# Slots 34 to 243 ordered by a list scheduler, solved in place in a ring of seven tiles

## The chip, the cores and the metric

The kernel runs on one core of a Trainium2 chip. The metric is the device time of one execution in microseconds (us). TensorE is called PE below, VectorE DVE, ScalarE ACT, GpSimd POOL and SyncE SP, as in the profile.

## The reference

```python
B, S, D = 16, 2048, 1024
xw = x @ w                              # x: B x S x D, w: D x D, float32
out[:, 0, :] = xw[:, 0, :]
for t in range(1, S):
    out[:, t, :] = decay[None, :] * out[:, t - 1, :] + xw[:, t, :]
```

A matrix product, and then along the time axis a decayed running sum with one decay for each of the 1024 columns.

## The kernel before, in words

**Tiling.** Time is cut into 64 chunks of 512 steps. Two chunks of one batch entry make a group, and the 1024 output columns are 8 tiles of 128. A *slot* is one group and one column tile: slot s = 8 * group + n, its result 128 columns by 1024 steps. A slot takes 16 matmuls of 128x512 on PE (8 blocks of the inner dimension, two chunks) into one of three PSUM tiles `ps0` to `ps2` of two banks each. Slots 0 to 247 are such; the last two chunks make 16 slots of half the length, so there are 264.

**Input.** A chunk is loaded in four quarters (`load`, L101) by DMAs that POOL issues, cast to bf16 on the way, into one of three `xb` tiles. DVE transposes the chunk in 32x32 blocks (`turn`, L110), one instruction of 128x2048, into one of two `xw` tiles. ACT copies it apart in two halves (`part`, L119; "X" and "Y" in the agenda) into one of five `xt` tiles, which PE reads. The quarters of later chunks wait in a list `loads`, which `turn_and_load` (L408) lengthens by those of chunk c + 3 when chunk c is turned.

**Solving a slot.** A *paired* slot halves the length of the serial scan:

- `copy` (p, ACT L183): PSUM to a tile `xs`, one of three
- `odd` (g, ACT L169): decay times the even steps, PSUM to a tile `h`, one of four
- `zero` (z, POOL L190 or ACT L192): the carry into column 1 of `so`, one of four
- `join` (j, POOL L196): odd steps of `xs` plus `h`, in place
- `scan` (S, DVE L201): 512 steps with decay squared, from `xs` into `so`
- `even` (h, ACT L169) and `fill` (c, POOL L246): the even steps, from `so` and `xs` into `so`
- `save` (k, ACT L250): the last step, for the same columns of the next group
- `back` (B, DVE L258): 32x32 transposes of `so` into a tile `ot`, one of four

A slot that is not paired has one DVE scan over all 1024 steps straight from PSUM (L221; D here), then save and back. Every fourth slot is of this kind (L149), apart from `flips`. Four slots, a *lump*, fill one `ot` tile; after the lump's last back, SP issues four stores of 512 KB.

A PSUM tile is free again when copy and odd have read it, or the long scan. So slot s + 3 cannot begin on PE before slot s has been read out.

**The order.** Each engine executes its instructions in the order in which the kernel writes them (`pin`). For slots 0 to 33 and the last 20 the order is written out by hand, slot by slot, in `agenda` (L447 to L503). For the slots between, `usual` (L514) writes the same pattern for every slot: pair of s, scans, completion of s - 1, backs of s - 2, then the turns and parts that `later` (L505 to L512) has put there, then one load or, if more than four are waiting, two. Slot 244 begins with `rest` (L528), which finishes slots 242 and 243.

Of the kernel before, what the change touches and what calls it, by code (L numbers as in the profile page):

```python
# [2 lines left out]

# [6 lines left out]
FP32 = mybir.dt.float32  # L10
BF16 = mybir.dt.bfloat16
ALU = mybir.AluOpType
# [13 lines left out]
def kernel(  # L26
# [26 lines left out]
    nc = tc.nc  # L53
    pin = tc.keep_in_program_order
    B, S, D = x.shape
    assert w.shape == (D, D)

    NQ = 4
    P = 32
    CQ = D // NQ  # L60
    K = CQ // P
    M = K // 2
    TL = 512
    NJ = TL // P
    NC = S // TL
    R = K // 2
    CH = D // 2
    CR = CH // NQ

    const = ctx.enter_context(tc.tile_pool(name="const", bufs=1))  # L70
    sb = ctx.enter_context(tc.tile_pool(name="sb", bufs=1))
# [4 lines left out]
    def ring(pool, name, count, shape, dtype=FP32):  # L76
        i = turns[name] = turns.get(name, -1) + 1
        return pool.tile(shape, dtype, name=f"{name}{i % count}")
# [13 lines left out]
    wcols = wsb.rearrange("p k (h r) q i -> p k h q r i", h=2)  # L92

    def ot_tile(nj):
        return ring(sb, "ot", 4, [128, nj, CR])

    xb_of = {}
    xw_of = {}
# [19 lines left out]

    def part(c, copy, m0, m1, j0=0, j1=NJ):  # L119
        if c not in xt_of:  # L120
            xt_of[c] = ring(sb, "xt", 5, [128, M, 2, TL], BF16)
        src = xw_of[c][:, m0:m1, j0:j1].rearrange("p m j i e -> p m e (j i)")
        pin(copy(out=xt_of[c][:, m0:m1, :, j0 * P:j1 * P], in_=src))  # L123

# [16 lines left out]
    class Tile:  # L141
# [3 lines left out]
        def __init__(self, g, n, ps, outlets):  # L145
            self.b, self.t0 = chunks[g[0]]
            self.T = TL * len(g)
            self.n, self.ps, self.outlets = n, ps, outlets
            self.paired = n % R != R - 1  # L149
            if len(tiles) in flips or len(tiles) - len(slots) in flips:  # L150
                self.paired = not self.paired
            self.turn = len(tiles)
            self.lot = sum(t.paired for t in tiles)
            self.prev = None if self.t0 == 0 else last[n]
            if self.t0 + self.T < S:
                last[n] = const.tile([128, 1], FP32, name=f"keep{n}", bufs=2)
                self.keep = last[n]
            else:
                self.keep = None

        @property
        def so(self):
            if not hasattr(self, "held"):
                self.held = sb.tile([128, 2 * TL + 2], FP32, name=f"so{self.turn % 4}")
            return self.held

        def decayed(self, src):
            h = ring(sb, "h", 4, [128, TL])[:, 0:self.T // 2]
            pin(nc.scalar.activation(  # L169
                out=h, in_=src, func=mybir.ActivationFunctionType.Copy,  # L170
                scale=dec[:, self.n:self.n + 1]))
            return h
# [6 lines left out]
                self.join()  # L179

        def copy(self):
            self.xs = sb.tile([128, 2 * TL], FP32, name=f"xs{self.lot % 3}")[:, 0:self.T]
            pin(nc.scalar.copy(out=self.xs, in_=self.ps))  # L183

        def odd(self):
            self.g = self.decayed(self.ps[:, 0:self.T:2])

        def zero(self):
            if self.prev is None:
                pin(nc.gpsimd.memset(self.so[:, 1:2], 0.0))  # L190
            else:
                pin(nc.scalar.copy(out=self.so[:, 1:2], in_=self.prev))  # L192

        def join(self):
            odds = self.xs[:, 1:self.T:2]
            pin(nc.gpsimd.tensor_tensor(out=odds, in0=self.g, in1=odds, op=ALU.add))  # L196

        def scan(self):
            T, n, so = self.T, self.n, self.so
            if self.paired:  # L200
                pin(nc.vector.tensor_tensor_scan(  # L201
                    out=so[:, 3:T + 2:2],
                    data0=squares[-1][:, n:n + 1].to_broadcast([128, T // 2]),
                    data1=self.xs[:, 1:T:2],
                    initial=0.0 if self.prev is None else self.prev,
                    op0=ALU.mult,
                    op1=ALU.add,
                ))
            else:
                parts = self.ps if isinstance(self.ps, tuple) else (self.ps,)  # L210
                size = T // len(parts)
                for i, ps in enumerate(parts):
                    self.run(ps, i * size, size)

        def run(self, ps, t, size):
            n, so = self.n, self.so
            if t:
                before = so[:, t + 1:t + 2]
            else:
                before = 0.0 if self.prev is None else self.prev  # L220
            pin(nc.vector.tensor_tensor_scan(  # L221
                out=so[:, t + 2:t + 2 + size],
                data0=dec[:, n:n + 1].to_broadcast([128, size]),
                data1=ps,
                initial=before,
                op0=ALU.mult,
                op1=ALU.add,
            ))
# [5 lines left out]
        def complete(self):  # L234
            if self.paired:
                self.even()
                self.fill()
            if self.keep is not None:
                self.save()

        def even(self):
            self.h = self.decayed(self.so[:, 1:self.T + 1:2])

        def fill(self):
            T = self.T
            pin(nc.gpsimd.tensor_tensor(  # L246
                out=self.so[:, 2:T + 2:2], in0=self.h, in1=self.xs[:, 0:T:2], op=ALU.add))

        def save(self):
            pin(nc.scalar.copy(out=self.keep, in_=self.so[:, self.T + 1:self.T + 2]))  # L250

        def back(self, half=None):
# [13 lines left out]
    class Outlet:  # L266


        def __init__(self, ns, nj, half=0, queues=(nc.sync,), pieces=1):
            self.pieces = pieces  # L270
            self.ns, self.missing, self.half = ns, set(ns), half
            self.nj, self.t0, self.queues = nj, half * nj * P, queues
            self.ot = ot_tile(nj)

        def store(self, b, t0):
            n0 = self.ns[0]
# [131 lines left out]
    def turn_and_load(c):  # L408
# [58 lines left out]
        18: "g16 T7 L h15 j16 p17 g17 B14 z17 c15 X7",  # L467
        19: "S16 j17 p18 B15 L g18 L S17 k16 h16 z18 j18",
        20: "Y7 S19 L c16 k17 h17 T8 k19 L c17",
        21: "p20 g20 L S18 X8 j20 B17 B19",  # L470
        22: "L h18 p21 c18 B16 k18 g21 B18 Y8 z20 L j21 S20",
        23: "p22 z21 z22 S21 L h20 g22 T9 c20 h21",
        24: "k21 k20 j22 S23 X9 L c21 Y9 B20 L",
        25: "B23 k23 p24 B21 g24 z24 j24 S22 z25",
        26: "p25 T10 k22 h22 g25 c22 S24 X10 j25",
        27: "B22 p26 S25 g26 z26 Y10 j26",
        28: "S27 h25 h24 c25 S26 c24",
        29: "B27 h26 c26 T11 p28 g28 j28 B24",
        30: "p29 B25 g29 z28 j29 S28 z29 S29",
# [22 lines left out]
        -1: "S-2 h-4 c-4 a-1 b-1 V",  # L502
    }  # L503
    flips = (1, 13, 15, -19, -18, -11, -8, -6, -3, -2)
    later = {}  # L505
    begun = {"T": 12, "X": 11, "Y": 11}
    for c in range(5, nch):
        first = c // 2 * K
        ahead = (7, 6, 4) if c % 2 else (11, 10, 8)
        for letter, a in zip("TXY", ahead):  # L510
            if c >= begun[letter]:
                later.setdefault(first - a, []).append(f"{letter}{c}")  # L512

    def usual(s):  # L514
        paired = [t.paired for t in tiles]
        do = [f"P{s}"] if paired[s] else []
        if paired[s - 1]:
            do.append(f"S{s - 1}")
        if not paired[s]:
            do.append(f"S{s}")  # L520
        do.append(f"C{s - 1}")
        if paired[s - 2]:
            do.append(f"B{s - 2}")
        if not paired[s - 1]:
            do.append(f"B{s - 1}")
        return do + later.get(s, []) + ["L"] * (2 if len(loads) > NQ else 1)

    def rest(s):  # L528
        do = [f"S{s - 1}"] if tiles[s - 1].paired else []
        do.append(f"C{s - 1}")  # L530
        if tiles[s - 2].paired:
            do.append(f"B{s - 2}")
        return do + [f"B{s - 1}"] + later.get(s, []) + ["L"] * len(loads)

    def perform(do):
        for deed in do:
            deeds[deed[0]](int(deed[1:] or 0))

    perform(agenda[-99].split())
    spares = [spare] + [ring(psp, "spare1", 1, [128, TL])]  # L540
    for step, (g, n) in enumerate(slots):
        T = TL * len(g)
        left = step - len(slots)
        if n % R == 0:
            ns, nj = range(n, n + R), T // P
            outlets = [Outlet(ns, nj)]
        if left == -R:
            outlets = []
        if step == 0:
# [48 lines left out]
            for k, l in todo:  # L598
                matmul(ps[:, l * TL:(l + 1) * TL], n, k, xt_of[g[l]])
        tiles.append(Tile(g, n, ps, outlets))  # L600
        do = agenda.get(step, agenda.get(left) if left >= -20 else None)
        if do is None:
            do = usual(step)
        else:
            do = do.split()
            if left == -20:
                do = rest(step) + do
        perform(do)
    assert not loads
# [1 line left out]
_INS = ['x', 'w', 'decay']  # L611
# [26 lines left out]
```

## Time and profile before

| | us |
|---|---|
| Median of 3 runs (lowest, highest) | 905.87 (905.47, 905.98) |
| The profiled execution's own time | 905.42 |
| Its span, first to last instruction | 903.5 |
| PE busy in the span | 892.3 |
| DVE, ACT, POOL busy | 825.5, 686.1, 657.2 |

In the profile, busy time is the time in which an engine executed at least one instruction. A group line names source line, engine, operation, what is written and read, the count, the busy time, the mean of one in ns, and the idle time ahead of it with what ended it. The timeline gives start, length and, in brackets, the idle time before an instruction and its releaser. The time from a DMA's issue to its landing is told by the views of one tile's instructions. An instruction often begins some 0.08 us before the recorded end of the one before it on the same engine.

### The profile page before, as it was taken

The numbers are of one execution on the slowest core, as the hardware profiler recorded it, in microseconds if no ns is written. First come the engines' busy times: TensorE is split into PE (matmuls) and PEld (weight loads), VectorE is DVE, ScalarE is ACT, GpSimd is POOL, SyncE is SP. The second block draws the span as 40 slices with busy tenths as digits, with TensorE's granted clock in tenths as the row PEclk, the third lists the DMA queues.
The fourth block names the chain that finished last, engine by engine and source line by source line (L and its number), as shares of the span: only waits on it lengthen the run. The fifth ranks groups of instructions, "written<-read, shape, count | busy, mean of one in ns | idle before, by whom it ended". The sixth has DMA issues, their size and how long they took to land.

```text
span 903.5 us, 11998 instructions
## 1 busy us (share of the span) xinstructions
PE 892.3 (99%) x4119; PEld 411.1 (45%) x4201; DVE 825.5 (91%) x628; ACT 686.1 (76%) x955; POOL 657.2 (73%) x755
## 2 busy tenths in 40 slices
PE   9999999999999999999999999999999999999997
PEld 5444444444444444444444444444444444444444
DVE  4999999999999999999998999999999999999997
ACT  4889867777877877877778778778777787787742
POOL 8888678777767768777677677787777776776632
PEclk9999999999999999999999999999999999999999
DMA  9999999999999999999999999999999999999868
GB/s 194 196 215 217 232 214 214 215 240 245 253 256 256 248 247 255 249 238 231 225 236 229 223 232 230 228 227 228 229 228 226 234 233 221 227 232 210 175 144 233
DMA packets 402542, 204.77 MB, mean 227 GB/s; under 512 B 8752, under 2 KB 401456, under 8 KB 402480
## 3 DMA queue, kind: packets, MB, share of 16 engines
q1 hardware_dynamic: 265168, 134.76, 61.1%
q0 software_dynamic: 137024, 68.70, 56.6%
q8 instruction: 33, 0.54, 0.2%
q10 hardware_dynamic: 288, 0.52, 0.2%
q14 instruction: 29, 0.24, 0.1%
HBM read 138.42 MB, written 134.22 MB: 302 GB/s over the span
## 4 chain that ended last, share of the span: by engine, by line
PE 94%; DMA 1%; DVE 1%; issue 1%; POOL 1%; ACT 0%; DVEq 0%; POOLq 0%
PE ps L131 94%; DMA ot<-in_w_dram 1%; DMA xb<-in_x_dram 1%; PE spare L131 1%; POOL xb L105 1%; DVE so L221 1%; POOL ot L299 0%; DVE xw L115 0%; ACT xt L123 0%; DVE ot L258 0%; PE spare L387 0%; DVE so L201 0%; DVE wsb L306 0%; ACT xs L183 0%; PE ps L387 0%
## 5 line engine op out<-in xcount | busy, mean ns | idle before, releaser
L131 PE MATMUL ps<-xt,wsb 128*128 128x512 bf16 x3942 | 863.5, 378 | 4.7 <-DVE wsb L306 0.3
L131 PEld LDWEIGHTS <-wsb 128*128 128x128 bf16 x4152 | 405.8, 98 | 480.0 <-ACT wsb L306 0.8
L196 POOL TENSOR_TENSOR xs<-h,xs 128x512 f32<-128x512 f32 (+1 forms) x190 | 242.9, 1278 | 189.5 <-ACT h L169 84.8
L183 ACT COPY xs<-ps 128x1024 f32<-128x1024 f32 (+1 forms) x190 | 189.4, 997 | 156.4 <-PE ps L131 146.2
L258 DVE STREAM_TRANSPOSE ot<-so 128x1024 f32<-128x1024 f32 (+1 forms) x260 | 300.1, 1192 | 3.1 <-POOL so L190 1.1
L246 POOL TENSOR_TENSOR so<-h,xs 128x512 f32<-128x512 f32 (+1 forms) x190 | 241.4, 1272 | 42.5 <-ACT h L169 27.9
L123 ACT COPY xt<-xw 128x2048 bf16<-128x2048 bf16 (+1 forms) x136 | 242.3, 1790 | 7.8 <-DVE xw L115 7.8
L105 POOL DMA_DIRECT2D xb<-in_x_dram x264 | 174.4, 662 | 3.2 <-DMA ot<-in_w_dram 1.0
L169 ACT ACTIVATE h<-so,dec 128x512 f32<-128x512 f32 (+1 forms) x190 | 145.4, 766 | 26.9 <-DVE so L201 23.7
L115 DVE STREAM_TRANSPOSE xw<-xb 128x2048 f32<-128x2048 f32 (+1 forms) x78 | 147.4, 1901 | 5.8 <-DMA xb<-in_x_dram 5.8
L201 DVE TENSOR_TENSOR_SCAN so<-spare,keep,xs 128x512 f32<-128x512 f32 (+1 forms) x97 | 120.0, 1240 | 27.5 <-POOL xs L196 27.2
L201 DVE TENSOR_TENSOR_SCAN so<-spare,xs 128x512 f32<-128x512 f32 x93 | 113.3, 1220 | 26.5 <-POOL xs L196 23.7
L169 ACT ACTIVATE h<-ps,dec 128x512 f32<-128x512 f32 (+1 forms) x190 | 130.2, 685 | 0.0
L221 DVE TENSOR_TENSOR_SCAN so<-dec,ps 128x1024 f32<-128x1024 f32 x34 | 76.8, 2261 | 1.0 <-ACT h L169 1.0
L221 DVE TENSOR_TENSOR_SCAN so<-dec,keep,ps 128x1024 f32<-128x1024 f32 (+1 forms) x35 | 76.0, 2171 | 0.2 <-issue 0.2
L250 ACT COPY keep<-so 128x1 f32<-128x1 f32 x136 | 25.4, 189 | 9.5 <-DVE so L221 9.0
L192 ACT COPY so<-keep 128x1 f32<-128x1 f32 x97 | 18.5, 191 | 2.5 <-DVE ot L258 2.3
L131 PE MATMUL ps<-xw,wsb 128*128 128x256 bf16 (+1 forms) x68 | 11.2, 301 | 0.0
L190 POOL MEMSET so<- 128x1 f32 x93 | 10.7, 116 | 0.6 <-DVE ot L258 0.6
L131 PE MATMUL spare<-xt,wsb 128*128 128x512 bf16 (+1 forms) x48 | 10.0, 335 | 0.0
L299 POOL DMA_DIRECT2D ot<-in_w_dram x12 | 6.6, 546 | 2.8 <-DMA xb<-in_x_dram 1.6
L324 PE MATMUL spare<-idle 128*128 128x512 bf16 x22 | 6.9, 488 | 1.2 <-DVE idle L314 1.2
(37 smaller groups left out, 36.5 us busy)
## 6 DMA issues: line engine op xcount, KB each, us to landing
out_dram<-ot SPq DMA_DIRECT2D x248, 512.0 KB, 10.9
xb<-in_x_dram POOLq DMA_DIRECT2D x248, 256.0 KB, 7.8
out_dram<-ot SPq DMA_DIRECT2D x12, 256.0 KB, 4.7
xb<-in_x_dram POOLq DMA_DIRECT2D x16, 128.0 KB, 5.6
ot<-in_w_dram POOLq DMA_DIRECT2D x12, 128.0 KB, 5.1
out_dram<-xb SPq DMA_DIRECT2D x3, 256.0 KB
ot<-in_w_dram ACTq DMA_DIRECT2D x2, 256.0 KB, 4.7
ot<-in_w_dram SPq DMA_DIRECT2D x2, 256.0 KB, 4.4
```

The source lines that it names most:

```text
L105: pin(nc.gpsimd.dma_start(out=xb_of[c][quad(q), j0:j1], in_=_ap(x, [[D, P], [P * D, j1 - j0], [1, CQ]], (b * S + t0 + j0 * P) * D + q * CQ)))
L115: pin(nc.vector.transpose(out=dst.rearrange("p (m j i) -> p j m i", m=M, i=P)[:, j0:j1, m0:m1], in_=src.rearrange("p (j m c) -> p j m c", ...
L123: pin(copy(out=xt_of[c][:, m0:m1, :, j0 * P:j1 * P], in_=src))
L131: pin(nc.tensor.matmul(out=ps[:, t0:t1] if ps.shape[1] >= t1 else ps, lhsT=lhs, rhs=rhs, start=(k == 0 and t0 == start), stop=(k == K - 1),))
L169: pin(nc.scalar.activation(out=h, in_=src, func=mybir.ActivationFunctionType.Copy, scale=dec[:, self.n:self.n + 1]))
L183: pin(nc.scalar.copy(out=self.xs, in_=self.ps))
L196: pin(nc.gpsimd.tensor_tensor(out=odds, in0=self.g, in1=odds, op=ALU.add))
L201: pin(nc.vector.tensor_tensor_scan(out=so[:, 3:T + 2:2], data0=squares[-1][:, n:n + 1].to_broadcast([128, T // 2]), data1=self.xs[:, 1:T:2 ...
L221: pin(nc.vector.tensor_tensor_scan(out=so[:, t + 2:t + 2 + size], data0=dec[:, n:n + 1].to_broadcast([128, size]), data1=ps, initial=befor ...
L246: pin(nc.gpsimd.tensor_tensor(out=self.so[:, 2:T + 2:2], in0=self.h, in1=self.xs[:, 0:T:2], op=ALU.add))
L250: pin(nc.scalar.copy(out=self.keep, in_=self.so[:, self.T + 1:self.T + 2]))
L258: pin(nc.vector.transpose(out=outlet.ot[:, :, c0:c0 + P], in_=self.so[:, 2 + t0:2 + t0 + nj * P].rearrange("p (i t) -> p i t", t=P)))
```

## The change

**Order.** Steps 34 to 243 are no longer written slot by slot. `steady` makes a `Job` for each piece of work: a quarter of a slot's matmuls, a copy, a scan, a load. A job has an engine, a cost, a key (when it is due, in us from the start of slot 34), and the jobs that it comes after. `in_order` then goes through time: whenever an engine has nothing to do, it gets the ready job with the lowest key. The jobs are emitted in order of these planned starts. The plan begins with all four engines idle at time 0. Its constants: 0.2158 us per matmul, 0.15 us from one engine to another, 19 us from a load's issue to its use, 13 us from a lump's last back to the free `ot` tile, and the costs in the dictionary below.

**Slots.** Every fifth slot (38, 43, ... 243) has the long scan; before it was every fourth (35, 39, ... 243). The code for `merged` groups has no effect: the tuple is empty, and every slot keeps its 16 matmuls.

**Turns and loads.** A chunk is turned in two DVE instructions of half the size (128 x 1024), each followed by its part on ACT. A load is planned no earlier than a slot after the one before it.

**Tiles.** `xs` is gone: copy, join, scan and fill work in `so`, which now has seven tiles. `xt` has four tiles in place of five, `ot` three in place of four, and these numbers hold for the whole kernel. An `ot` tile is taken at a lump's first back.

**Ahead of slot 34.** In the agenda, the parts of chunks 8 and 9 stand 1 to 3 steps later; those of chunk 10 have left step 26 and 27 for the scheduler. At slot 34 the scheduler also takes over scan, save, even, fill and back of slot 33 and the back of slot 32.

```diff
+    OTS, XTS, SOS, HS = 3, 4, 7, 4
+    FROM, TO = 34, 244
+    merged = ()
...
-        21: "p20 g20 L S18 X8 j20 B17 B19",
-        22: "L h18 p21 c18 B16 k18 g21 B18 Y8 z20 L j21 S20",
+        21: "p20 g20 L S18 j20 B17 B19",
+        22: "L h18 p21 c18 B16 k18 g21 B18 z20 L j21 S20",
         23: "p22 z21 z22 S21 L h20 g22 T9 c20 h21",
-        24: "k21 k20 j22 S23 X9 L c21 Y9 B20 L",
-        25: "B23 k23 p24 B21 g24 z24 j24 S22 z25",
-        26: "p25 T10 k22 h22 g25 c22 S24 X10 j25",
-        27: "B22 p26 S25 g26 z26 Y10 j26",
+        24: "X8 k21 k20 j22 S23 Y8 L c21 B20 L",
+        25: "B23 k23 p24 B21 g24 z24 j24 S22 X9 z25",
+        26: "p25 T10 k22 h22 g25 c22 Y9 S24 j25",
+        27: "B22 p26 S25 g26 z26 j26",
...
+    cost = {"p": 1.01, "g": .69, "z": .15, "j": 1.3, "S": 1.24, "D": 2.28, "h": .77, "c": 1.3,
+            "k": .19, "B": 1.21, "T": 1.19, "X": 1.9, "L": .66, "half": .585, "both": .68, "sum": 1.2, "wpool": 1.15, "wdve": .4, "slow": 4.2}
...
+        def chunk(c):
+            need = starts[c // 2] - 18 + (c % 2) * 12
+            if c > 11:
+                quads = [q for cc, q in loads if cc == c] if c <= 14 else range(NQ)
+                got = [Job("pool", cost["L"], need - 28 + 2.5 * q, lambda c=c, q=q: load(c, q),
+                           [turned.get(c - 3)]) for q in quads]
+                for q, a in zip(quads, got):
+                    a.early = max(0.0, need - 3 * 4 * each * R + 2 + q * each * R)
+                ends = [(a, LAND) for a in got]
+                for half in range(2):
+                    turned[c] = Job(
+                        "dve", cost["T"], need + 2 * half,
+                        lambda c=c, h=half: turn(c, 0, NJ, h * M // 2, (h + 1) * M // 2),
+                        ends + [turned.get(c - 1), part_of.get((c - 2, 1)), turned.get(c)])
+                    part_of[c, half] = Job(
+                        "act", cost["X"], need + 3 + 3 * half,
+                        lambda c=c, h=half: part(c, nc.scalar.copy, h * M // 2, (h + 1) * M // 2),
+                        [turned[c], part_of.get((c - 1, half))] + used.get(c - XTS, []))
...
+        def solve(tile, ready, key, banks):
...
+            gone = place.get((s - SOS, "B"))
...
+                end = pos("S", "dve", "D", 0, tile.scan, ready + [gone, prev])
...
+                    p = pos("p", "act", "p", 0, tile.copy, ready + [gone])
...
+                g = pos("g", "act", "g", .5, None, ready, True)
...
+                j = pos("j", "pool", "j", 1.2, tile.join, ready_xs + [g])
+                j.gives = (g,)
+                S = pos("S", "dve", "S", 1.5, tile.scan, [j, prev])
+                h = pos("h", "act", "h", 4.5, None, [S, z], True)
...
+                end = pos("c", "pool", "c", 4.4, tile.fill, [h])
...
+            if tile.kept:
+                pos("k", "act", "k", 3.7, tile.save, [place[s, "S"]])
+            back(tile, end, key)
...
+            b = Job("dve", cost["B"], key + 5, tile.back,
+                    [end, place.get((s, "k"))] + stored.get(lump - OTS, []) + ([first] if first else []))
...
+                last_one = Job("pe", each, t + q * each, do,
+                               [part_of.get((c, q // 2)) for c in g] + [last_one]
+                               + (after_ps[bank - 3] if bank >= 3 and q == 0 else []))
...
+        order = in_order()
+        for job in order:
+            job.do()
```

Of the built kernels, these stretches of each engine's order matter below (letters as above, numbers are slots; L, T and X with the chunk, its two parts a and b; L12 is issued in four quarters).

```
before, DVE   S33 B32 S34 D35 B33 B34 B35 S36 T12 S37 B36 S38 D39
after,  DVE   S33 B32 T12a B33 T12b S34 S35 B34 S36 B35 D38 S37 B36
before, ACT   p33 g33 h32 k32 p34 g34 h33 k33 X11a h34 k34 p36 g36 k35 X11b p37 g37
after,  ACT   p33 g33 h32 k32 X10a k33 h33 X10b p34 g34 X11a p35 g35 k34 h34 p36 g36 X11b k35 h35 p37 k36 g37
before, POOL  z32 j32 L12 L12 z33 j33 c32 L12 L12 z34 j34 c33 L13 L13 c34
after,  POOL  z32 j32 L12 L12 z33 j33 c32 L12 L12 L13 c33 z34 L13 j34 z35 L13 j35 c34 z36 j36 L13 c35
both,   DVE   D23 B20 B23 B21 S22 T10 S24 B22 S25 D27 S26 B27 T11 B24 B25 S28 S29 B26 B28 D31 S30 B29 B30 B31 S32 S33
```

## The prediction

> **What bounds the kernel now.** I read the page's busy line and the chain that ended last, then that chain in order of time.
>
> ```profile
> PE 892.3 (99%) x4119; PEld 411.1 (45%) x4201; DVE 825.5 (91%) x628; ACT 686.1 (76%) x955; POOL 657.2 (73%) x755
> ...
> PE 94%; DMA 1%; DVE 1%; issue 1%; POOL 1%; ACT 0%; DVEq 0%; POOLq 0%
> ```
>
> ```profile
> 47.87 10.74 PE ps L131 x49
> ...
> 69.67 10.74 PE ps L131 x49
> 80.46 10.74 PE ps L131 x49
> ...
> 857.67 10.74 PE ps L131 x49
> ```
>
> Piece by piece, from 41 to 868 us, the chain is PE alone: 50 matmuls (one record in 50 is missing) per 10.79 us, 0.2158 each, 3.453 a slot. PE never waits in slots 34 to 243, and the change leaves it every matmul. So there is **nothing to gain there**: the change is worth what it makes PE wait, and PE runs to the end, so every such microsecond is added. Slot 33 ends at 129.65 (its copy, waiting for PE, starts at 129.71); from there slot ends follow by 3.453.
>
> PE is covered by three PSUM tiles: slot s + 3 begins when copy and odd (or the long scan) of slot s are done. That is where I look for waits.
>
> **The steady part costs nothing, I estimate.** Pitches (start to start in the timelines): scan 1.14, long scan 2.18, back 1.16, copy 0.91, odd 0.58, even 0.67, part 1.83, join and fill 1.25, load 0.66. A half turn (128x1024) has no row; it lies between half of the whole turn's 2.2 and a back of equally many elements, 1.10 to 1.16; I take 1.13. Scan and join in place have no row either; the nearest are the two forms of the scan, 1.22 and 1.28, so within 0.06 either way; same taken. Five slots take 17.27 us. DVE then has 4 scans, a long scan, 5 backs, 2.5 half turns = 15.4; ACT 4 x 2.16 + 2.5 x 1.83 + 0.4 of small copies = 13.6; POOL 4 x 2.5 + 5 x 0.66 + 0.2 = 13.5. Each fits with 10% or more to spare, and the planner's costs (1.21 a back, 1.01 a copy) are above the pitches.
>
> **What goes wrong is the seam.** Two things meet there.
>
> 1. *Three `ot` tiles.* Back 20 opens lump 5 and now needs lump 2's tile, not lump 1's. The last of lump 2's stores is issued by SP at 83.49:
>
> ```profile
> DMA to landing us min/median/max: 18.4/18.4/18.4
> ```
>
> It lands at 101.9. The DVE timeline has back 20 at 98.66:
>
> ```profile
> 98.66 3.46 DVE L258 STREAM_TRANSPOSE ot<-so 128x1024 f32<-128x1024 f32 x3
> ...
> 132.72 1.22 DVE L201 TENSOR_TENSOR_SCAN so<-spare,xs 128x512 f32<-128x512 f32 x1 [0.70 <-POOL xs L196]
> 134.23 1.25 DVE L258 STREAM_TRANSPOSE ot<-so 128x1024 f32<-128x1024 f32 x1 [0.28 <-POOL so L246]
> ...
> 145.43 2.31 DVE L115 STREAM_TRANSPOSE xw<-xb 128x2048 f32<-128x2048 f32 x1 [0.71 <-DMA xb<-in_x_dram]
> ```
>
> So DVE waits 3.3 us, and from 98.66 to 127 it has no gap to make this up. The long scan of slot 31 begins at 125.9, not 122.75, and ends at 128.1, before slot 34 needs its tile at 129.65: PE loses nothing yet. Through scan 30, even 30, copy and odd 32 (ACT) and join 32 (POOL) the delay reaches the first load of chunk 12: 133.0, not 129.94.
>
> 2. *The turn of chunk 12.* In `chunk`, c = 12 finds no quarter in `loads` (the agenda issued all four just ahead), so the plan has the turn wait for no landing. Its first half stands behind back 32, ahead of back 33, scans 34 and 35; before, the turn stood behind scan 36 and even so waited 0.71 (last line above). In that stretch landings take
>
> ```profile
> DMA to landing us min/median/max: 8.0/11.9/14.6
> ```
>
> The first quarter landed 8.0 after its issue, at 137.9, the last, issued at 134.8, 10.5 later at 145.3: 2.46 apart. From 133.0 this gives 133.0 + 8.0 + 7.4 = **148.4**. Back 32 ends at 138.4: DVE stands still for 10 us, and behind the turn wait scan 34, then on ACT save 34 and, behind it in order, copy 36.
>
> Slot by slot, with ACT's new order:
> - Scan 33 ends at 137.0 (join 33 is late too). Parts 10, now here, keep 33 and even 33 put copy 34 at 140.3; odd 34 ends at 141.9. Slot 37 begins at 142.0, not 139.95: **2.0**.
> - From 148.45: half turn, back 33, half turn, scan 34 until 153.1; even 34, copy 36, odd 36 until 155.5. Slot 39 begins at 155.6, not 146.9: **8.7** in all.
> - Slot 40 needs odd 37, behind part 11b, even 35, copy 37: 159.75. Slot 39 at full clock ends at 159.05: 0.7 more.
> - *Clock.* PE has then been idle for 6.7 us. The trace shows what PE does after rest: its first nine matmuls of this size start 0.427 apart, then 0.216; that is 2.0 us lost. And it shows the clock going down after rest: PE's last matmul is at 898.3, and in the last microsecond the granted clock is 0.73.
>
> ```profile
> 1.20 6.91 PE L324 MATMUL spare<-idle 128*128 128x512 bf16 x22 [1.20 <-DVE idle L314]
> ```
>
> ```profile
> 902.50:903.50 1.00, 0.00 (x0) 0.00 (x0) 0.00 (x0) 0.00 (x0) 0.00 (x0) 0.73 0.00 0
> ```
>
> I count the 2.0, in place of the 0.7, which it covers: slot 40 begins at 161.1, not 150.4, **10.7 late**. The price lies between the 0.7 (no fall) and some 3.4, a whole cold slot.
> - Long scan 38 ends at 162.9, slot 41 needs it at 164.5; copy 40 and odd 40 end before slot 43 asks at 171. Walked on by hand until slot 48, nothing more waits; part 13b, the tightest, ends 1.0 ahead of its use.
>
> At the other end, slot 244, the last fill and back of slot 242 come no later than the next long scan can start: nothing. Later stores have 32 us from a lump's last back to the first back three lumps on; from 400 us on they need 15.
>
> Sum, on the profiled execution (905.42, 1.9 of it around the span): 905.42 + 10.7 = **916.1**. The median of the runs lies 0.45 above that execution.
>
> The Trainium skill ("DMA: Bandwidth & Descriptors", section "Anatomy of one DMA — SWDGE (gpsimd) path") fits a POOL-issued load as 2.0 us plus bytes over 436 GB/s, 2.6 for 256 KB, an estimate by which the wait at the turn would nearly vanish (rival d). The trace's 8.0 to 14.6 speak against it here, with stores queued on the same engines.
>
> **Rivals.**
> (a) *The clock doesn't fall* in one wait of 6.7: 8.7 + 0.7, 914.8.
> (b) *The wait at back 20 is made up* before slot 34, so chunk 12 lands at 145.3 and slot 37 is on time: slot 39 loses 5.7, and 0.7 to 2.0 follow: 911.8 to 913.1. Against: DVE has no gap there.
> (c) *The stores keep DVE waiting.* Lump 8's four stores were issued from 157.2 to 176.2, after its last back at 143.6; landed 190.2. Lump 11's first back would come at some 187 and wait 3, and the next two lumps like it: 2 to 5 more, 918 to 921. Against: POOL's loads stand behind even 34 too and come up to 16 later, so stores drain faster.
> (d) *Not slower.* The three PSUM tiles cover the wait. From the turn's start to odd 36's end are 7.1 us and slot 39 is due at 146.9, so it decides itself at a turn start of 139.7, with odd 34 by 139.9. The last quarter would have to land 2 us after its issue at 137.8; then 905.4. Landing after 2.6, the turn would start at 140.4, as part 10b ends, odd 36 end at 147.5, and only the 2.0 at slot 37 remain: 907.4. No 256 KB load of the trace after 200 us landed in under 6.4.
> (e) *A part comes late at each group:* 26 groups at 0.5 us, 13 more, 929. Against: the 1.0 above.
> (f) *The change doesn't do what it says:* the built order has turns, loads and seven tiles as described; only chunk 12 is turned without its loads in the plan. (If the order had stayed, 905.4.)
>
> **Chances.** Forecast 45, (a) 18, (b) 13, (c) 11, (e) 5; (d) 6, of which 2 are the 907.4; faster 2 (only start or tail could give it, and neither is edited). The range 911.5 to 920 holds the forecast, (a), (b) and part of (c), some eight in ten. A measurement here tells 0.2%, 1.8 us, from no change: slower 94, within 4, faster 2.
>
> **What would show it.** In the changed profile: DVE idle some 3 us ahead of a back near 98.7, ended by `out_dram<-ot`; idle some 10 us ahead of a half turn at about 148, ended by `xb<-in_x_dram`; PE waiting at about 140 and 149 for ACT's odd copies, the nine matmuls after it 0.43 apart; then PE unbroken to the end. A PE that waits in later slots, or a turn that begins before 142, would make this wrong.

## The result and the profile after

| | before | after |
|---|---|---|
| Median, us (lowest to highest) | 905.67 (905.46 to 905.98) | 916.71 (915.85 to 919.42) |
| Ratio, 95% interval | | 1.0128 (1.0116 to 1.0140) |
| Profiled execution, us | 905.42 | 916.68 |

The changed kernel is slower by 11 us; the forecast was 916.1. First the busy line of its page and the chain that ended last:

```profile
PE 899.9 (98%) x4201; PEld 411.7 (45%) x4201; DVE 812.8 (89%) x680; ACT 703.0 (77%) x993; POOL 684.3 (75%) x783
...
PE 82%; DVE 4%; DMA 2%; issue 2%; SPq 1%; POOL 1%; ACT 1%; POOLq 0%; DVEq 0%; ACTq 0%
```

PE has gone from 94% of the chain to 82%: somewhere the chain leaves PE. PE's timeline from 136 to 166 us shows where (start, length, then in brackets the wait ahead):

```profile
142.53 7.07 PE L138 MATMUL ps<-xt,wsb 128*128 128x512 bf16 x32 [1.72 <-ACT h L184]
155.49 10.69 PE L138 MATMUL ps<-xt,wsb 128*128 128x512 bf16 x38 [5.90 <-ACT h L184]
```

Two waits, ahead of slots 37 and 39. Before them, from start-up on, and after them, up to the last matmul of the product, the run is unbroken. The chain in order of time gives the way into the second:

```profile
138.52 9.82 DMA xb<-in_x_dram
...
148.46 0.06 DVE xw L122
...
149.63 1.20 DVE ot L273
150.84 1.13 DVE xw L122
151.96 1.12 DVE so L216
...
153.30 0.66 ACT h L184
153.96 0.89 ACT so L197
154.85 0.60 ACT h L184
...
155.49 10.69 PE ps L138 x38
```

That is the last quarter of chunk 12, its half turn, back 33, the other half turn, scan 34, then on ACT even 34, copy 36, odd 36, then slot 39. DVE's timeline has both of the stops that the forecast counted on, in their places:

```profile
102.65 3.50 DVE L273 STREAM_TRANSPOSE ot<-so 128x1024 f32<-128x1024 f32 x3 [3.28 <-DMA out_dram<-ot]
...
126.52 2.30 DVE L236 TENSOR_TENSOR_SCAN so<-dec,keep,ps 128x1024 f32<-128x1024 f32 x1
...
148.46 1.25 DVE L122 STREAM_TRANSPOSE xw<-xb 128x1024 f32<-128x1024 f32 x1 [9.26 <-DMA xb<-in_x_dram]
```

The four loads of chunk 12, issued from 133.67, took

```profile
DMA to landing us min/median/max: 7.6/8.6/9.8
```

And the clock, in stretches after the second wait (the column after POOL's is the granted clock):

```profile
157.00:161.00 4.00, 4.00 (x12) 1.47 (x11) 2.70 (x3) 3.21 (x7) 3.12 (x5) 0.59 0.60 70
161.00:165.00 4.00, 4.00 (x21) 1.82 (x19) 4.00 (x4) 2.17 (x5) 2.93 (x5) 1.00 0.76 132
```

From 157 to 161 PE is busy without a break, but has 12 matmuls under way where the next stretch has 21.

**Where every microsecond is.** One of the experiments below (e8, profiled at 905.72) has no wait on PE after start-up, and no matmul record is missing in its trace or in that of the changed kernel. So the two can be set side by side, matmul by matmul. The changed kernel is 0.38 us late from start-up on and stays so up to slot 36; 2.25 late at the first matmul of slot 37 (1.87 more), 8.31 at slot 39 (6.06 more), 10.64 at slot 40 (2.33 more, 11 matmuls 0.427 apart in place of 0.216). At the last matmul of the product, 746 us later, it is 10.64 late: nothing is lost or made up in between. A little more is lost only behind that. Ahead of the transposes that PE does at the very end, it waits 0.38 for POOL's last fill, and they start 11.06 late. In the traces here this wait is 0.37 to 0.43 in the changed order with three `ot` tiles, 0.19 to 0.20 with four, and absent in the old order; no run traces it further.

### The profile page after: what moved, and what is told of

The parts are those of the page before. It is cut to its first block, busy times and chain, and to the rows that moved or that the text cites. A ratio compares the mean times of both kernels' runs of the same rounds, so it can differ in the third digit from the quotient of the medians.

```text
span 914.9 us, 11913 instructions
## 1 busy us (share of the span) xinstructions
PE 899.9 (98%) x4201; PEld 411.7 (45%) x4201; DVE 812.8 (89%) x680; ACT 703.0 (77%) x993; POOL 684.3 (75%) x783
## 4 chain that ended last, share of the span: by engine, by line
PE 82%; DVE 4%; DMA 2%; issue 2%; SPq 1%; POOL 1%; ACT 1%; POOLq 0%; DVEq 0%; ACTq 0%
PE ps L138 81%; DVE ot L273 1%; DMA out_dram<-ot 1%; DVE xw L122 1%; DMA xb<-in_x_dram 1%; SPq L302 1%; DVE so L216 1%; PE spare L138 1%; ACT h L184 0%; POOL so L261 0%; POOL so L211 0%; ACT so L197 0%; PE spare L407 0%; PE ps L407 0%; DVE so L236 0%
## 5 line engine op out<-in xcount | busy, mean ns | idle before, releaser
L261 POOL TENSOR_TENSOR so<-h,so 128x512 f32<-128x512 f32 (+1 forms) x201 | 256.9, 1279 | 125.0 <-ACT h L184 113.3
L211 POOL TENSOR_TENSOR so<-h,so 128x512 f32<-128x512 f32 (+1 forms) x201 | 257.7, 1282 | 82.4 <-ACT h L184 33.0
L197 ACT COPY so<-ps 128x1024 f32<-128x1024 f32 (+1 forms) x201 | 200.6, 998 | 123.7 <-PE ps L138 123.5
L184 ACT ACTIVATE h<-so,dec 128x512 f32<-128x512 f32 (+1 forms) x201 | 154.9, 771 | 26.7 <-DVE so L216 26.7
L122 DVE STREAM_TRANSPOSE xw<-xb 128x1024 f32<-128x1024 f32 (+2 forms) x130 | 154.1, 1194 | 14.2 <-DMA xb<-in_x_dram 14.2
L216 DVE TENSOR_TENSOR_SCAN so<-spare,keep,so 128x512 f32<-128x512 f32 (+1 forms) x102 | 124.6, 1224 | 16.4 <-POOL so L211 16.1
L184 ACT ACTIVATE h<-ps,dec 128x512 f32<-128x512 f32 (+1 forms) x201 | 138.0, 686 | 0.0
L216 DVE TENSOR_TENSOR_SCAN so<-spare,so 128x512 f32<-128x512 f32 x99 | 118.8, 1203 | 11.5 <-POOL so L211 11.4
L236 DVE TENSOR_TENSOR_SCAN so<-dec,keep,ps 128x1024 f32<-128x1024 f32 (+1 forms) x30 | 64.6, 2152 | 10.3 <-PE ps L138 10.1
L236 DVE TENSOR_TENSOR_SCAN so<-dec,ps 128x1024 f32<-128x1024 f32 x28 | 63.5, 2271 | 7.7 <-PE ps L138 7.3
L205 POOL MEMSET so<- 128x1 f32 x99 | 10.5, 108 | 0.0
```

The source lines that it names most:

```text
L122: pin(nc.vector.transpose(out=dst.rearrange("p (m j i) -> p j m i", m=M, i=P)[:, j0:j1, m0:m1], in_=src.rearrange("p (j m c) -> p j m c", ...
L184: pin(nc.scalar.activation(out=h, in_=src, func=mybir.ActivationFunctionType.Copy, scale=dec[:, self.n:self.n + 1]))
L197: pin(nc.scalar.copy(out=self.line, in_=self.ps))
L216: pin(nc.vector.tensor_tensor_scan(out=so[:, 3:T + 2:2], data0=squares[-1][:, n:n + 1].to_broadcast([128, T // 2]), data1=so[:, 3:T + 2:2] ...
L236: pin(nc.vector.tensor_tensor_scan(out=so[:, t + 2:t + 2 + size], data0=dec[:, n:n + 1].to_broadcast([128, size]), data1=ps, initial=befor ...
L261: pin(nc.gpsimd.tensor_tensor(out=evens, in0=self.h, in1=evens, op=ALU.add))
```

## The experiments

The theory on trial: there are two causes, the third `ot` tile and the turn of chunk 12 that the plan puts ahead of its loads' landing, both at the seam of slot 34, and the 210 slots that the scheduler orders cost nothing. The main rival: the stores, with three `ot` tiles, keep DVE waiting (c). All times are medians; the kernel before, measured beside them, had 905.26 to 905.70.

| run | edit | us | ratio to before (95%) |
|---|---|---|---|
| e1 | changed kernel, four `ot` tiles | 914.77 | 1.0104 (1.0089 to 1.0119) |
| e2 | changed kernel, turn of chunk 12 later | 907.79 | 1.0029 (1.0018 to 1.0040) |
| e3 | both | 905.78 | 1.0006 (0.9997 to 1.0016) |
| e4 | changed kernel, PE kept busy in the long wait | 916.22 | 1.0119 (1.0103 to 1.0136) |
| e6 | e1 with the same | 913.51 | 1.0096 (1.0081 to 1.0111) |
| e7 | changed kernel without stores of lumps 3 to 6 | 915.36 | 1.0114 (1.0098 to 1.0129) |
| e10 | without stores of lumps 3 to 9 | 912.06 | 1.0069 (1.0052 to 1.0086) |
| e5 | kernel before, three `ot` tiles | 913.40 | 1.0091 (1.0074 to 1.0108) |
| e8 | e5 with one load per step | 905.56 | 1.0003 (0.9994 to 1.0012) |
| e9 | e2 without the spacing of loads | 931.19 | 1.0259 (1.0217 to 1.0302) |

### e1, e2, e3: the two causes, one at a time

e1 gives the tile back, e2 puts the turn where its loads have landed, e3 does both.

```diff
-    OTS, XTS, SOS, HS = 3, 4, 7, 4
+    OTS, XTS, SOS, HS = 4, 4, 7, 4
```

```diff
                         ends + [turned.get(c - 1), part_of.get((c - 2, 1)), turned.get(c)])
+                    if c == 12 and half == 0:
+                        turned[c].early = 20.0
```

> The changed kernel with four ot tiles again; everything else as changed. Theory (two waits meet at slot 34: three ot tiles hold DVE for 3.3 us at back 20, and the turn of chunk 12 stands ahead of its landing): the 3.3 us wait at back 20 is gone, so chunk 12's last quarter lands 3 us earlier, slot 37 loses nothing (2.0 before), slot 39 loses about 5.7 and the cold matmuls 2.0 more: about 913 us, 3 to 4 below the changed kernel. Rival (the ot tiles don't matter, the turn does it all): 916 to 917, as changed.

> The changed kernel, but the turn of chunk 12 is planned no earlier than 20 us after the start of slot 34; three ot tiles as changed. The stop of DVE at the turn and the 6 us wait of PE at slot 39 go in both theories. Theory A (the seam is all): PE keeps at most the 2 us at slot 37, 905.5 to 908. Theory B (the stop had hidden a second cost of three ot tiles: without it the stores of lumps 7 to 9, which in the kernel before land 40 to 47 us after the lump's last back, hold up the first backs of lumps 10 to 13 by up to 14 us): 909 to 917, with DVE idle for several us ahead of backs, ended by stores, between 165 and 230 us.

> Both edits together: four ot tiles, and the turn of chunk 12 no earlier than 20 us after the start of slot 34. Theory (these two are the whole loss): PE has no wait after 42 us, 905.3 to 906.5, within 0.2% of the kernel before. Rival (the scheduler's order costs PE time elsewhere too, a little at each group): 908 or more, with PE waits spread over the span.

PE's timeline around the seam, in e1:

```profile
136.76 10.31 PE L138 MATMUL ps<-xt,wsb 128*128 128x512 bf16 x46
153.96 12.24 PE L138 MATMUL ps<-xt,wsb 128*128 128x512 bf16 x44 [6.89 <-ACT h L184]
```

in e2:

```profile
141.57 24.77 PE L138 MATMUL ps<-xt,wsb 128*128 128x512 bf16 x112 [1.06 <-ACT h L184]
```

and in e3:

```profile
136.80 29.52 PE L138 MATMUL ps<-xt,wsb 128*128 128x512 bf16 x134
```

Each edit takes away its own wait and leaves the other: with four tiles back 20 starts at 98.6, slot 37 is on time and slot 39 is not; with the later turn it is the other way round. From the changed kernel's 916.71, e1 gains 1.94, e2 8.92, both 10.93, which is their sum within 0.1 (the kernel before had 905.67 beside the one and 905.26 beside the others). e3 can't be told from the kernel before, since its interval holds 1. So these two are the loss, and the scheduler's order, the ring of seven and the slots solved in place cost at most some 0.2%; of that, e3's trace shows the 0.20 at the tail. e1 was expected lower, since chunk 12's loads begin earlier in it; but the last of them, issued at 135.0, took 11.8 us to land where the kernel before has 10.5, and slot 39 waited 7.05 (from start to start, less the 0.216 of a matmul; the timeline's 6.89 runs from the recorded end). e2 also decides against rival (c): after back 20, DVE never waits for a store.

### e4, e6: what the fallen clock costs

24 matmuls on zeros, into a PSUM bank that nobody reads, fill PE's wait ahead of slot 39, in the changed kernel (e4) and with four tiles (e6).

```diff
+                    if q == 0 and s == 39:
+                        warm = psp.tile([128, TL], FP32, name="spare0")
+                        for _ in range(24):
+                            pin(nc.tensor.matmul(out=warm, lhsT=idle[:, 0:128], rhs=idle, start=True, stop=True))
```

> The changed kernel with 24 matmuls of zeros (5.2 us at full clock) on a spare PSUM bank ahead of slot 39, where PE waits for about 6.1 us; their result is not used. Theory (PE's rest lets the clock fall, which costs some 2 us beyond the wait): the clock stays up, slot 39 begins when it did, its matmuls start 0.216 apart, and slot 40 then waits 0.7 for its PSUM tile: 1.3 to 1.9 us below the changed kernel, about 915. Rival (the slow matmuls come from something else than the rest): the same 916 to 917 with slow matmuls in slot 39, or longer by up to 5 if the fillers delay it.

> The changed kernel with four ot tiles (which had one PE wait, 7.05 us ahead of slot 39, then 12 matmuls at half speed, and 914.77), and 24 matmuls on a tile of zeros put on PE ahead of slot 39, into a PSUM bank that nobody reads. They add 24 x 0.216 = 5.2 us (at most 10.2 if all run at half speed) of work inside a wait of 7. Theory A (the half-speed matmuls after the wait are a cost of their own: 12 x 0.211 = 2.5 us, less what slot 40 would have waited anyway, 0.7): 912.5 to 913.3, no matmul 0.427 apart after slot 39 starts. Rival (slot 40's wait takes the place of the slow matmuls in full): 914.4 to 915.2.

PE's timeline, in e4:

```profile
142.11 8.75 PE L138 MATMUL ps<-xt,wsb 128*128 128x512 bf16 x31 [2.14 <-ACT h L184]
150.70 5.34 PE L733 MATMUL spare<-idle 128*128 128x512 bf16 x24
157.05 3.61 PE L138 MATMUL ps<-xt,wsb 128*128 128x512 bf16 x16 [1.01 <-ACT h L184]
161.17 5.12 PE L138 MATMUL ps<-xt,wsb 128*128 128x512 bf16 x22 [0.51 <-ACT h L184]
```

and in e6:

```profile
153.73 3.61 PE L138 MATMUL ps<-xt,wsb 128*128 128x512 bf16 x16 [1.64 <-ACT h L184]
157.86 8.36 PE L138 MATMUL ps<-xt,wsb 128*128 128x512 bf16 x37 [0.51 <-ACT h L184]
```

In both, slot 39 now takes 3.6 us for its 16 matmuls, at full speed, and slot 40 then waits. The medians can't carry the verdict: chunk 12 landed 1.55 later in e4's profiled run than in the changed kernel's, and the intervals of e1 and e6 overlap. A distance inside each trace can. From slot 39's first matmul to the last one of the product it is 751.61 in the changed kernel and 751.65 in e1, 750.63 in e4 and 750.66 in e6. So the slow matmuls cost **1.0 us net**. Gross it is 2.33, but without them slot 40 waits 0.68 and two later slots 0.48 and 0.23 in e6. The theory is right in kind and too high (e6's expectation has 1.8); the rival, by which other waits take all of its place, is wrong.

e4 has something else. The first line is slots 37 and 38, 8.75 us for their matmuls (31 of 32 recorded), after a wait of 2.14: the clock fell there too. In the changed kernel the same slots took 7.07, after a wait of 1.72. (From start to start, less 0.216, these waits are 2.31 and 1.88.)

### e7, e10: why the loads take so long

The stores are left out for some lumps (their part of the output is not written), so that chunk 12 loads alone.

```diff
+            stores.append(self)
+            if 4 <= len(stores) <= 7:
+                return
```

In e10 the bound is 10 in place of 7.

> The changed kernel without the 16 stores of lumps 3 to 6 (their part of the output is not written); lump 2's stay, so that back 20 waits as before. No store is then under way while chunk 12 is loaded. Theory A (the loads take 9.8 us to land because stores share the 16 DMA engines with them): the last quarter of chunk 12, issued at about 138.5, lands 5 to 6 us later, the half turn begins at about 144, slot 39 waits some 2 us in place of 6, 908 to 911.5. Rival 1 (the time is the load's own, whatever else runs: the first quarter, with no load ahead of it, took 7.6 to 8.0): landing 9 to 10 after issue, 916 to 917. Rival 2, by the Trainium skill ("DMA: Bandwidth & Descriptors", section "Anatomy of one DMA — SWDGE (gpsimd) path"), an estimate from its fit: 2.6 us from issue to landing, half turn at about 141, only the 2 us at slot 37 left, 907.5.

> The run without the stores of lumps 3 to 6 left its question open: SP then issued lump 7's first store early, and it landed at 142.5, so only the first quarter of chunk 12 was loaded alone (5.0 us). Here the stores of lumps 3 to 9 are left out (their part of the output is not written), so that none is under way from 102 us until chunk 12 has landed. Theory A (stores and loads share the engines half and half, as 256 KB per 2.48 us and 512 KB per 4.85 us side by side suggest): alone, a load follows the one ahead of it by 1.2 to 1.5 us, the last quarter, issued at about 137.8, lands 5 to 6.5 us later, the half turn begins at 143 to 144.5, PE waits 1.5 to 3.3 us ahead of slot 39, 910 to 912.5. Theory B (a load of this kind takes 2.4 us in its queue whatever runs beside it): the last quarter lands 7.4 or more after its issue, the half turn begins at 145.2 to 147, slot 39 waits 4 to 6 us, 913.5 to 916.

e7 missed its aim. SP, freed of 16 stores, came to lump 7's early, and the first of these landed at 142.5, among the loads. Only the first quarter was loaded alone; it landed 5.0 after its issue, where the changed kernel has 7.6. So e7's nearness to rival 1 says nothing. e10 mends that. Its DMA view from 133 to 150 us, where only loads ran:

```profile
q0 software_dynamic: 3696, 1.84, 88.2%
...
xb<-in_x_dram POOLq DMA_DIRECT2D x7, 256.0 KB, 5.7
```

The last line gives the loads issued, their size and the median time to landing. The four quarters of chunk 12 landed 4.3, 5.3, 5.7 and 6.3 after their issue, and loads that queue behind one another 1.2 to 1.6 apart; the kernel before has 8.0 to 10.5, and 2.5 apart. PE:

```profile
143.02 8.75 PE L139 MATMUL ps<-xt,wsb 128*128 128x512 bf16 x32 [2.07 <-ACT h L185]
152.46 3.61 PE L139 MATMUL ps<-xt,wsb 128*128 128x512 bf16 x16 [0.69 <-ACT h L185]
```

Slot 39 waits 0.9 in place of 6.1, partly because here too the clock fell after the 2.2 us ahead of slot 37: slots 37 and 38 took 1.7 longer, which made slot 39 ask later. The landing and the 912.06 are in theory A's ranges. The half turn, at 145.42, and the wait are not: the last quarter was issued at 139.0, 1.2 later than the expectation had it, and the expectation left the clock out. So stores that share the engines with the loads cost the last quarter 3.5 of its 9.8 us; the other 6.3 are there without them.

### e5, e8, e9: when three tiles are too few

Rival (c) is false for the changed kernel. Is it false because three tiles are enough, or because of where its loads stand? e5 is the kernel before with three `ot` tiles; e8 adds that a step never issues two loads; e9 is e2 without the lines that set a load's earliest time.

```diff
-        return ring(sb, "ot", 4, [128, nj, CR])
+        return ring(sb, "ot", 3, [128, nj, CR])
```

```diff
-        return do + later.get(s, []) + ["L"] * (2 if len(loads) > NQ else 1)
+        return do + later.get(s, []) + ["L"]
```

```diff
-                for q, a in zip(quads, got):
-                    a.early = max(0.0, need - 3 * 4 * each * R + 2 + q * each * R)
```

> The kernel before, with nothing changed but three ot tiles in place of four. It asks whether the third tile's loss belongs to the tile alone, or to the tile together with the place of the loads. Theory A (the loads of the kernel before, issued in pairs from 130 us on, hold the stores up: in its trace lump 8's last store landed at 190.2, 46.6 after its last back, and by the landings of lumps 7 to 10 the first backs of lumps 10 to 13 would have to wait 9, 15, 13 and 13 us, most of it one and the same delay handed on): DVE waits up to 15 on out_dram<-ot around 165 to 215, PE loses what its three PSUM tiles do not cover, 8 to 11 us, 913 to 916. Theory B (only back 20 waits, 3.3 us at 98.7, and the PSUM tiles cover that as they did in the changed kernel up to slot 34): no PE wait after 41 us, 905.3 to 906.5.

> The kernel before with three ot tiles (913.4; DVE waited 3.3, 1.7 and 6.9 us on out_dram<-ot, PE 1.3, 0.5 and 5.7), and with one more edit: a step issues one load, never two. In the run without this edit the loads land 2.48 us apart from 143 to 192 us without a break, and in that stretch the 512 KB stores land 4.9 us apart; after it 1.5 to 3. Theory A (a load queue that never empties holds the stores back; the third tile costs only together with it): one load per 3.45 us leaves gaps, a lump's stores are landed some 24 to 30 us after its last back, the first back three lumps on comes 32 after it; DVE waits at back 20 only, 905.3 to 906.8. Theory B (the third tile is too few for any order of the loads, by the 4.9 us of a store): lags of lumps 7 to 10 stay above 32, PE waits of 5 and more near 170 to 190, 911 to 915. A risk to both: chunks 13 to 15 land later, and a turn near 160 to 185 waits for its load.

> The converse: the changed kernel with the turn of chunk 12 put later (907.79, no wait on stores after back 20), without the lines that space the loads by a slot. POOL's built order then has the loads of chunks 12, 13 and 14 nearly in one row, 12 loads between join 33 and join 34. Theory A: they land 2.48 apart for some 30 us from about 142, stores in that stretch some 4.9 apart in place of 2 to 5; lumps 7 and 8 land 5 to 10 us later than with spacing (161.5 and 177.0 there), which takes their lag to within a few us of the first back of lump 10 or 11; 908 to 912. Theory B (spacing does nothing for the stores): lumps 7 and 8 land within 2 us of 161.5 and 177.0, 907.2 to 908.5.

The waits (total, times, longest) in e5:

```profile
DVE ot L258 <- DMA out_dram<-ot: 11.9, 3, 6.9
...
PE ps L131 <- DVE so L221: 7.0, 3, 5.5
```

in e8:

```profile
DVE ot L258 <- DMA out_dram<-ot: 3.9, 2, 3.1
```

and in e9:

```profile
DVE ot L273 <- DMA out_dram<-ot: 56.8, 17, 7.4
```

One tile fewer costs the kernel before 8 us, and with one load per step nothing. The DMA views from 145 to 190 us say why. In e5 (packets, MB, share of the engines; then issues and median time to landing):

```profile
q0 software_dynamic: 9535, 4.73, 76.2%
q1 hardware_dynamic: 9831, 4.96, 53.2%
...
out_dram<-ot SPq DMA_DIRECT2D x10, 512.0 KB, 18.4
xb<-in_x_dram POOLq DMA_DIRECT2D x13, 256.0 KB, 13.0
```

and in e8:

```profile
q0 software_dynamic: 8142, 4.04, 66.1%
q1 hardware_dynamic: 13192, 6.65, 60.4%
...
out_dram<-ot SPq DMA_DIRECT2D x13, 512.0 KB, 12.9
xb<-in_x_dram POOLq DMA_DIRECT2D x14, 256.0 KB, 7.5
```

q0 carries the loads, q1 the stores. In e5 the load queue stays filled in this stretch (four to seven loads between issue and landing for 88% of it, and never fewer than two), and both queues move the same: 4.73 and 4.96 MB in 45 us, 105 and 110 GB/s. That is a load every 2.48 us and a store every 4.85, but the slots need four loads and four stores in 13.8 us, and four such stores take 19.4. The stores fall behind by some 5.6 us per lump until the loads have caught up (lump 8 lands 41 us after its last back); three tiles leave 32. In e8 two or three loads are between issue and landing for 90% of it, and the load queue's share of the engines falls from 76.2% to 66.1%; the stores move 6.65 MB in the same time, and lump 8 lands 29 us after its last back. The Trainium skill ("DMA: Bandwidth & Descriptors", section "Queues, rings and completion order") says that a DMA engine takes turns between its queues, a packet at a time. The equal shares of e5 agree with that; that the loads go 1.2 to 1.6 apart once the stores are gone (e10) does too.

e9 is slower by far more than expected, 931 where 908 to 912 was forecast, and not where the expectation placed it. The burst at chunks 12 to 14 keeps no back waiting for a store: after back 20, the first such wait ends at 246.76 and is 0.49 long. What the burst does is hold up POOL: seven loads stand ahead of fill 33 and ten ahead of join 34, and slots 37 and 39 wait 2.1 and 7.7 at the seam. Behind it the scheduler issues loads in bursts to the end (after 150 us, 88 of 196 follow the one before within 1 us; 35 of 199 in e2), and 16 more first backs wait for stores, up to 7.4 each. Matmul by matmul against e8, the profiled execution (937.06, the slowest of four from 924.53 on) loses 12.6 us up to slot 40, with the fallen clock, and 18.2 from there to the last matmul of the product. That the stores cause the second part is argued from the waits on them; no run takes it apart.

## Why the prediction was right, step by step

- **Nothing to gain, steady part free.** Right. e3 is at 1.0006, and the distance to e8 does not move from slot 40 to the last matmul of the product. The tail, which the forecast had at nothing, costs 0.4.
- **Three `ot` tiles, 3.3 at back 20.** Right: 3.28. Its way to slot 37 is right too: long scan 31 at 126.5 (125.9 forecast) and the first load of chunk 12 at 133.67 (133.0), both in an execution that is 0.84 later from start-up on than the trace from which the forecast was made; slot 37 1.87 late (2.0). e1 confirms that this is its cause, and that rival (b), a wait made up before slot 34, fails.
- **The turn ahead of its landing.** Right: DVE idle 9.26 (10), half turn at 148.46 (148.45), slot 39 6.06 (6.7). e2 confirms it. The landing met its time partly by luck: the loads began 0.7 later and took 0.7 less than forecast. PE had moved by the 0.84 of start-up and the landing had not, so slot 39's wait came out 0.6 shorter. In the profiled runs with this burst the last quarter took from 9.8 to 13.0 us, so this term was worth its number within 2 or 3.
- **The clock.** It fell, so rival (a) is wrong, and 2.33 gross stands against the 2.0. But the forecast put the price of no fall 1.3 lower, and e4 and e6 make it 1.0: not only slot 40 waits in place of the slow matmuls, two later slots do too. For this case the forecast has the first wait alone.
- **The sum.** 1.87 + 6.06 + 2.33 = 10.26, against 10.7. Beside e8, the profiled run adds 0.38 at start-up and 0.4 at the tail, which no step had; beside the trace of the kernel before, which the forecast started from, it is 0.84 and 0.4. In the twelve profiles the first matmul of the product starts between 10.5 and 11.3, so start-up varies by as much. Without the two, 905.42 + 10.26 would be 915.7: that 916.68 lies as near to 916.1 is luck in part.
- **Rival (c).** Wrong here, as the forecast leaned. Its reason, that the loads come later and the stores drain faster, fits: in the kernel before, lumps 8 to 16 land 34 to 47 us after their last back, in the changed kernel no lump from 8 on takes more than 23 of the 32 us that it has (the trace tells the landing of every second lump). In the old order of loads (c) is true and costs 8 us (e5), and by e8 it is the pace of the loads that decides there. For the changed order e9 shows less: without spacing, waits for stores come back, but from 246 us on and not at the lumps that (c) named. The forecast's "15" from 400 us on is 15 to 18 in the trace before; nothing hangs on it.
- **Rival (d).** Wrong, but the reason against it was half of the truth. The forecast held stores responsible for 8.0 to 14.6 us of landing. e10 shows a floor below that: without stores, 4.0 to 4.3 for a load with nothing ahead of it (3.9 and 5.0 in e7). So (d), which needed 2, fails even with the engines to itself; and the estimate of 2.6 by the Trainium skill's fit ("DMA: Bandwidth & Descriptors", section "Anatomy of one DMA — SWDGE (gpsimd) path") is not reached in any run here: the shortest load behind start-up took 3.8.
- **Rivals (e) and (f).** Wrong: no wait in later groups, and the built order did what the change says.

No run beat the kernel before. e3 and e8 equal it within their intervals, each with less of some tile; in all three PE is busy from start-up to the end of the product.

## What to carry to other kernels

Where a planner takes over from an order written by hand, look at what it does not know: here four loads issued just ahead of it, which its plan held to have landed, cost more than the 210 slots that it ordered well. How many buffers suffice is not a property of the buffers' users alone: count how long a store takes while the load queue is never empty, and see whether loads can be spaced before giving a buffer back or taking one away. To price a stall, compare two traces event by event up to the end; the distance that stays is the price, and a median that moves by another cause does not blur it.

## What the runs showed of the hardware

- **Two filled queues moved the same.** With both filled, 105 and 110 GB/s (e5); a store of 512 KB then landed every 4.85 us, and every 1.5 at the best with no load under way (171.8 to 176.3 us in e9). A load of 256 KB landed every 2.48 us beside stores, every 1.2 to 1.6 without them (e10).
- **A wait of 2.2 us was enough for the clock to fall.** Counted from start to start, less 0.216, the waits at which it went to 0.5 are 2.23 (e10), 2.31 (e4), 2.77 and 3.99 (e9) and all of 5.46 and more; at none of 1.2 to 2.11 (e9) did it fall. In e4 the window of 144 to 146 us reads:

```profile
144.00:146.00 2.00, 2.00 (x6) 0.76 (x5) 0.00 (x0) 1.34 (x2) 0.66 (x2) 0.50 1.30 216
```

  By the traces' own records of the clock it stays there for 3.41 us or a multiple: 3.41 in e4 and e10, 6.83 in e1 and the changed kernel, 10.24 in e9. The Trainium skill ("TensorE: Matmul & The Clock Gate", section "What's actually happening") has a free-running window of 3413 ns, which agrees; it has the clock fall after an idle window of about that length, and here a wait of 2.23 did it. Whether a wait's length decides alone, or also where it falls in such a window, these runs do not tell.
- **A cold restart can be cheaper than its slow matmuls,** 1.0 of 2.33 us here, because the engines that feed PSUM back use the time.
